# Sparse attention of a hybrid encoder: bias and mask are summed on GpSimd ahead of the logits

## The chip, the core and the metric

One NeuronCore of a Trainium2 chip runs the whole program in one launch. Its engines are TensorE (PE, matrix multiply; PEld is its weight load), VectorE (DVE), ScalarE (ACT), GpSimd (POOL) and SyncE (SP, here a queue for DMAs). Each works through its own instructions strictly in the order in which they stand in its queue, and waits on semaphores for the others. The metric is the device time of one execution in microseconds (us); the time of a version is the median of its runs.

## The reference, cut to what matters

Two layers of an encoder on a sequence of 512 positions of width 1024, all in float32. Each layer projects its normalised input with one wide matrix, feeds four mixers (a state-space scan, a sparse attention, an RWKV-7 recurrence and a diagonal state-space model called S5), gates and sums their outputs, and ends in a feed-forward block. The change lies in the sparse attention:

```python
score = jnp.where(admissible[None], score, -jnp.inf)
sel_score, sel_idx = lax.top_k(score, top_k)          # 128 keys of 512 for each query
...
logits = jnp.einsum("bqhd,bqkhd->bqhk", qb, k_sel).astype(f32) * dh ** -0.5
logits = logits + jnp.transpose(rel_bias[bucket], (0, 1, 3, 2)).astype(f32)
logits = jnp.where(valid[:, :, None, :], logits, -jnp.inf)
probs = jax.nn.softmax(logits, axis=-1)
return jnp.einsum("bqhk,bqkhd->bqhd", probs.astype(v.dtype), v_sel)
```

There are 8 heads of 64 columns. A query sees only keys of its own chunk of 64 and of earlier chunks.

## The kernel before

Nothing is gathered. The kernel computes the logits of each block of 128 queries against all keys up to the block's end, and adds a mask that holds 0 where a key is among the chosen and 1e30 where it is not. All signs are turned over (queries are scaled by -1/8, the bias is stored negated), so the softmax's maximum is a minimum here, and the exponential takes scale -1.

The function `dsa` does a layer's attention. `dsa_scores` first makes the masks of query blocks qt = 1 to 3: sixteen pairs of a MAX (L708) and a MATCH_REPLACE (L709) on DVE take the 128 largest scores of each query, and L710 writes the mask. The main loop then runs over four pairs of heads (hp) and four query blocks (qt); a step is one (hp, qt), has W = 128, 256, 384 or 512 keys, and does the two heads e = 0 and 1 of the pair. For each head:

- PE: logits into PSUM tile `lgp` (L656).
- DVE: `lg` = logits + bias (L661), then one custom operation that adds the mask and takes the row minimum `mn` (L662, TENSOR_TENSOR_REDUCE, which the trace calls CUSTOM_DVE_ANT_0 and the instruction order calls ISA).
- ACT: exponential with the row sum (L664). DVE: reciprocal (L670) and scaling (L671).
- PE: qt + 1 transposes into PSUM tile `ptp` (L674). ACT: copy of them to SBUF, `dspt` (L675). PE: product with the values, into `po` (L679).

Tiles `bias`, `lg` and some others share one ring of five buffers (tag Ta). The bias of a head is a DMA from DRAM issued by the POOL queue (L648). Logits of a step stand behind the last `po` product of the step before on PE, which the helper `behind` enforces.

The order of instructions on each engine isn't written by hand. A scheduler at build time lays out the program from priorities (attention and the other mixers stand above the large projections) and its own estimate of each operation's length. The projections fill PE wherever the mixers are not ready: `pj` (L302 to L304, three matrix multiplies for each pair of tiles, helper `mm3`) and `pgl`, the same lines used by the S5 mixer's gated unit (L1075 to L1077 are its operations on ACT and DVE). Their weights come by DMA into `raw`; ACT makes the rounded part `wh` (L295) and DVE the rest `wl` (L296). A `pj` or `pgl` multiply that stands on PE between an attention step's logits and its transposes is called a filler here.

Of the kernel before, what the change touches and what calls it, by code (L numbers as in the profile page):

```python
# [81 lines left out]
def ap_of(t, offset, dims):  # L82
    return bass.AP(tensor=t.tensor, offset=t.offset + offset, ap=[list(d) for d in dims])


class Trunk:
# [521 lines left out]
    def dsa(self, ar):  # L608
        nc = self.nc
        mm = nc.tensor.matmul  # L610
        self.misc_proj(ar)
        qs = self.A(ar + "0", [4, S], "dsq", F32R)
        qh, ql = self.T("dsqh", dt=F32R), self.T("dsql", dt=F32R)
        self.split_out(qh, ql, self.pin(C_QI))
        for j in range(4):
            for n, t in enumerate((qh, ql, qh)):
                nc.gpsimd.dma_start(qs[32 * n:32 * n + 32, j], t[32 * j:32 * j + 32])
        mask = self.mask
        moff = [0, 128, 384, 768]
        nc.gpsimd.memset(mask[:, :128], 0.0)  # L620
        nc.gpsimd.memset(mask[:64, 64:128], -NEG)
        yb = self.y_dram("ybd")
        qvs = []
        for hp in range(4):
            qv = self.A(f"{ar}{2 + hp}", [4, S], "qkvo")
            qvs.append(qv)
            q, k, vc = qv[:, 0], qv[:, 1], qv[:, 3]
            vt = qv[:, 2].rearrange("p (t c) -> p t c", c=128)
            nc.scalar.activation(q, self.pin(C_Q + hp * 128), AF.Copy, scale=-0.125)
            nc.scalar.copy(k, self.pin(C_K + hp * 128))  # L630
            nc.scalar.copy(vc, self.pin(C_V + hp * 128))
            pv = self.P("pv")
            for t in range(4):
                nc.tensor.transpose(pv[:, t * 128:(t + 1) * 128], vc[:, t * 128:(t + 1) * 128], self.ident)
            nc.scalar.copy(vt, pv.rearrange("p (t c) -> p t c", c=128))
        self.dsa_scores(qs, mask, moff)
        pts = self.A(ar + "0", [2, 2, S], "dspt")
        n, freed = 0, None
        for hp in range(4):
            qv = qvs[hp]  # L640
            q, k = qv[:, 0], qv[:, 1]
            vt = qv[:, 2].rearrange("p (t c) -> p t c", c=128)
            er = [slice(e * 64, e * 64 + 64) for e in range(2)]
            po = self.P("po")
            bias, mn, sm, rs = [], [], [], []
            for e in range(2):
                b_ = self.T("bias")
                self.q("bi").dma_start(b_, ap_of(self.relb, (hp * 2 + e) * 128 * 640 + 127, [[639, 128], [1, 512]]))  # L648
                bias.append(b_)
                for l, nm in ((mn, "mn"), (sm, "sm"), (rs, "rs")):  # L650
                    l.append(self.sp.tile([128, 4], F32, name=nm, bufs=4))
            for qt in range(4):
                W = 128 * (qt + 1)
                ps = [self.P("lgp") for _ in range(2)]
                for e in range(2):
                    i = mm(ps[e][:, :W], q[er[e], qt * 128:(qt + 1) * 128], k[er[e], :W], start=True, stop=True)  # L656
                    self.behind(i, freed)
                ts_ = [self.T("lg") for _ in range(2)]
                for e in range(2):
                    t = ts_[e]  # L660
                    nc.vector.tensor_add(t[:, :W], ps[e][:, :W], bias[e][:, 384 - 128 * qt:512])  # L661
                    nc.vector.tensor_tensor_reduce(t[:, :W], t[:, :W], mask[:, moff[qt]:moff[qt] + W], 1.0, 3e38,  # L662
                                                   op0=OP.add, op1=OP.min, accum_out=mn[e][:, qt:qt + 1])
                    nc.scalar.activation(t[:, :W], t[:, :W], AF.Exp, scale=-1.0, bias=mn[e][:, qt:qt + 1],  # L664
                                         accum_out=sm[e][:, qt:qt + 1])
                pt = pts[:, n % 2]
                n += 1
                for e in range(2):
                    t = ts_[e]
                    nc.vector.reciprocal(rs[e][:, qt:qt + 1], sm[e][:, qt:qt + 1])  # L670
                    nc.vector.tensor_scalar(t[:, :W], t[:, :W], rs[e][:, qt:qt + 1], None, op0=OP.mult)  # L671
                    pp = self.P("ptp")
                    for b in range(qt + 1):
                        nc.tensor.transpose(pp[:, b * 128:(b + 1) * 128], t[:, b * 128:(b + 1) * 128], self.ident)  # L674
                    nc.scalar.copy(pt[:, e, :W], pp[:, :W])  # L675
                freed = None
                for b in range(qt + 1):
                    for e in (1, 0):
                        i = mm(po[er[e], qt * 128:(qt + 1) * 128], vt[:, b, er[e]], pt[:, e, b * 128:(b + 1) * 128],  # L679
                               start=(b == 0), stop=(b == qt))  # L680
                        self.behind(i, freed)
                        freed = i
            t = self.T("ybt")
            nc.scalar.copy(t, po)
            self.y_store(yb, hp, t)
        self.dbg_y("yb", yb)
        return yb
# [911 lines left out]
```

## Time and profile before

| what | value |
|---|---|
| three timed runs | 2310.33, 2313.12, 2317.92 us (median 2313.12) |
| profiled execution, own time | 2318.86 us |
| its span, first to last instruction | 2317.1 us |
| PE busy | 2242.8 us, 97% of the span |
| DVE busy | 1448.4 us, 63% |
| ACT busy | 921.0 us, 40% |
| POOL busy | 103.6 us, 4% |

Busy time of PE counts a multiply from its start to the end of its pipeline, and neighbours overlap, so PE's real pace is read from starts of one multiply to the next. Attention takes place from about 175 to 365 us in the first layer and from about 1304 to 1498 us in the second.

### The profile page before, as it was taken

How to read it: one execution, taken by the hardware profiler on the slowest of the kernel's cores; microseconds unless marked ns; L12 is line 12 of the kernel's file. 1: busy time of each engine (PE TensorE's matmuls, PEld its weight loads, DVE VectorE, ACT ScalarE, POOL GpSimd, SP SyncE). 2: the span in 40 equal slices, each digit the busy share in tenths (PEclk: the TensorE clock that was granted, in tenths of full speed). 3: DMA queues.
4: the chain of work that ended last, by engine and by line, in shares of the span. 5: the costliest groups of instructions: out<-in, count | busy, mean ns of one | idle time of the engine just before them, and what ended most of it. 6: DMA issues, size and time to landing. Idle time of an engine off the chain costs nothing.

```text
span 2317.1 us, 32591 instructions
## 1 busy us (share of the span) xinstructions
PE 2242.8 (97%) x12660; PEld 1789.5 (77%) x12660; DVE 1448.4 (63%) x2676; ACT 921.0 (40%) x1455; POOL 103.6 (4%) x180
## 2 busy tenths in 40 slices
PE   6999999999999999999999999999999999999998
PEld 5777777777778888887878777687777888888786
DVE  5669867767678587543244696568668775444333
ACT  5443464244642343322233335533456333222232
POOL 3320000000000101000012000000000000000000
PEclk9999999999999999999999999999999999999999
DMA  7444552444166435433365445443333653333332
GB/s 219 114 104 128 144 170 80 116 101 124 55 205 204 119 92 166 125 97 105 111 187 150 123 124 168 123 101 105 91 110 106 222 160 91 100 97 95 89 98 86
DMA packets 429186, 290.08 MB, mean 125 GB/s; under 512 B 65024, under 2 KB 386768, under 8 KB 427432
## 3 DMA queue, kind: packets, MB, share of 16 engines
q1 hardware_dynamic: 419520, 261.45, 39.3%
q0 software_dynamic: 8512, 26.43, 4.1%
q8 instruction: 99, 1.62, 0.3%
q14 instruction: 55, 0.45, 0.1%
q10 hardware_dynamic: 1000, 0.13, 0.0%
HBM read 237.30 MB, written 51.43 MB: 125 GB/s over the span
## 4 chain that ended last, share of the span: by engine, by line
PE 81%; DVE 11%; DMA 4%; issue 2%; ACT 2%; SPq 0%; DVEq 0%; ACTq 0%; POOLq 0%
PE pj L303 16%; PE pj L304 16%; PE pj L302 16%; PE pf L304 3%; PE pf L302 3%; PE pf L303 3%; PE pb L302 3%; PE pb L303 3%; PE pb L304 3%; DVE wl L296 2%; DMA rnd<-rwrn 1%; PE lgp L656 1%; PE ptp L674 1%; PE po L679 1%; DVE score L709 1%
## 5 line engine op out<-in xcount | busy, mean ns | idle before, releaser
L302 PE MATMUL pj<-hh,wh 128*128 128x512 f32 x1888 | 750.1, 398 | 11.0 <-DVE conv L1453 4.9
L304 PE MATMUL pj<-hh,wl 128*128 128x512 f32 x1888 | 749.7, 397 | 0.4 <-DVE wl L296 0.4
L303 PE MATMUL pj<-hl,wh 128*128 128x512 f32 x1888 | 749.7, 397 | 0.1
L295 ACT CAST wh<-raw 128x1024 fp32r<-128x1024 f32 x336 | 348.6, 1037 | 922.6 <-PE pj L303 344.3
L296 DVE TENSOR_TENSOR wl<-raw,wh 128x1024 fp32r<-128x1024 f32 x336 | 405.2, 1206 | 350.8 <-ACT wh L295 348.9
L302 PEld LDWEIGHTS pj<-hh,wh 128*128 128x128 f32 x1888 | 356.3, 189 | 91.0 <-issue 8.6
L303 PEld LDWEIGHTS pj<-hl,wh 128*128 128x128 f32 x1888 | 356.4, 189 | 81.7 <-issue 9.0
L304 PEld LDWEIGHTS pj<-hh,wl 128*128 128x128 f32 x1888 | 356.0, 189 | 79.1 <-issue 6.3
L302 PE MATMUL pf<-hid,wh 128*128 128x512 f32 x352 | 137.9, 392 | 1.6 <-ACT wh L295 1.6
L304 PE MATMUL pf<-hid,wl 128*128 128x512 f32 x352 | 137.7, 392 | 0.5 <-DVE wl L296 0.5
L303 PE MATMUL pf<-hid,wh 128*128 128x512 f32 x352 | 136.9, 390 | 0.0
L302 PE MATMUL pb<-yh,wh 128*128 128x512 f32 x256 | 100.9, 394 | 0.0
L303 PE MATMUL pb<-yl,wh 128*128 128x512 f32 x256 | 100.8, 394 | 0.0
L304 PE MATMUL pb<-yh,wl 128*128 128x512 f32 x256 | 100.3, 392 | 0.0
L536 DVE TENSOR_TENSOR fa<-fa,pj 128x512 f32<-128x512 f32 x44 | 30.2, 688 | 95.3 <-PE pj L304 95.2
L533 DVE TENSOR_TENSOR fa<-pj,rb 128x512 f32<-128x512 f32 x44 | 30.4, 691 | 88.6 <-PE pj L304 88.6
L302 PEld LDWEIGHTS pf<-hid,wh 128*128 128x128 f32 x352 | 66.1, 188 | 16.8 <-ACT wh L295 3.4
L304 PEld LDWEIGHTS pf<-hid,wl 128*128 128x128 f32 x352 | 66.1, 188 | 16.0 <-DVE wl L296 2.6
L303 PEld LDWEIGHTS pf<-hid,wh 128*128 128x128 f32 x352 | 66.1, 188 | 13.4
L664 ACT ACTIVATE lg<-lg,mn 128x128 f32<-128x128 f32 (+3 forms) x64 | 35.8, 559 | 61.6 <-DVE mn L662 60.0
L302 PEld LDWEIGHTS pb<-yh,wh 128*128 128x128 f32 x256 | 48.1, 188 | 10.7 <-DVE m L476 0.7
L303 PEld LDWEIGHTS pb<-yl,wh 128*128 128x128 f32 x256 | 48.1, 188 | 9.8
(493 smaller groups left out, 2977.5 us busy)
## 6 DMA issues: line engine op xcount, KB each, us to landing
raw<-in_w_in SPq DMA_DIRECT2D x146, 512.0 KB
raw<-in_ffn_w SPq DMA_DIRECT2D x120, 512.0 KB
gates<-gate SPq DMA_DIRECT2D x64, 256.0 KB
gld<-gates SPq DMA_DIRECT2D x64, 256.0 KB
raw<-in_w_branch SPq DMA_DIRECT2D x32, 512.0 KB
raw<-in_w_out SPq DMA_DIRECT2D x16, 512.0 KB
raw<-in_ffn_w SPq DMA_DIRECT2D x16, 384.0 KB
bias<-relb POOLq DMA_DIRECT2D x16, 256.0 KB, 3.1
```

The lines of the kernel that those rows point to most:

```text
L295: nc.scalar.copy(wh[:, :n], raw[:, :n])
L296: nc.vector.tensor_sub(wl[:, :n], raw[:, :n], wh[:, :n].bitcast(F32))
L302: mm(ps, wh, ah, start=first, stop=False)
L303: mm(ps, wh, al, start=False, stop=False)
L304: mm(ps, wl, ah, start=False, stop=last)
L533: nc.vector.tensor_mul(a, p1, rb)
L536: nc.vector.tensor_mul(a, a, p3)
L656: i = mm(ps[e][:, :W], q[er[e], qt * 128:(qt + 1) * 128], k[er[e], :W], start=True, stop=True)
L664: nc.scalar.activation(t[:, :W], t[:, :W], AF.Exp, scale=-1.0, bias=mn[e][:, qt:qt + 1], accum_out=sm[e][:, qt:qt + 1])
L674: nc.tensor.transpose(pp[:, b * 128:(b + 1) * 128], t[:, b * 128:(b + 1) * 128], self.ident)
L679: i = mm(po[er[e], qt * 128:(qt + 1) * 128], vt[:, b, er[e]], pt[:, e, b * 128:(b + 1) * 128], start=(b == 0), stop=(b == qt))
L709: nc.vector.match_replace(sc[:, :W], m8, sc[:, :W], PICK)
```

## The change

The sum that no longer needs the logits goes first, and to another engine. GpSimd adds the bias and the mask into the step's `lg` tile. DVE's custom operation then adds the logits from PSUM to it and takes the minimum; DVE's own addition is gone. The sums are formed in another order, with the same operands.

```diff
                 for e in range(2):
                     t = ts_[e]
-                    nc.vector.tensor_add(t[:, :W], ps[e][:, :W], bias[e][:, 384 - 128 * qt:512])
-                    nc.vector.tensor_tensor_reduce(t[:, :W], t[:, :W], mask[:, moff[qt]:moff[qt] + W], 1.0, 3e38,
+                    nc.gpsimd.tensor_add(t[:, :W], bias[e][:, 384 - 128 * qt:512], mask[:, moff[qt]:moff[qt] + W])
+                    nc.vector.tensor_tensor_reduce(t[:, :W], ps[e][:, :W], t[:, :W], 1.0, 3e38,
                                                    op0=OP.add, op1=OP.min, accum_out=mn[e][:, qt:qt + 1])
                     nc.scalar.activation(t[:, :W], t[:, :W], AF.Exp, scale=-1.0, bias=mn[e][:, qt:qt + 1],
```

The scheduler lays the program out anew around this; outside the two stretches of attention and some 130 us behind each, the order is the same. Three places show what moves.

On POOL, the first layer. Before, the eight bias loads (two for each pair of heads) stand one behind the other:

```order
L1013 DMA s5T<-ktd 16x16x16
L648 DMA bias<-relb 128x512 x8
L1211 MEMSET NZ 64x32 x2
```

In the changed kernel the additions stand between them (here the first two pairs of heads; the ISA row is there once in the program):

```order
L648 DMA bias<-relb 128x512 x2
L661 ISA
L661 TENSOR_TENSOR lg<-bias,mask 128x128 x2
L661 TENSOR_TENSOR lg<-bias,mask 128x256 x2
L661 TENSOR_TENSOR lg<-bias,mask 128x384 x2
L661 TENSOR_TENSOR lg<-bias,mask 128x512 x2
L648 DMA bias<-relb 128x512 x2
L661 TENSOR_TENSOR lg<-bias,mask 128x128 x2
L661 TENSOR_TENSOR lg<-bias,mask 128x256 x2
```

So a pair's bias loads are issued only behind the eight additions of the pair before, and an addition stands behind the bias loads of its own pair.

On DVE, the step of 256 keys of the first layer's last pair of heads. Before:

```order
L661 TENSOR_TENSOR lg<-lgp,bias 128x256 x2
L662 ISA lg,mn<-lg,mask 128x256
L662 ISA mn 128x1
L662 ISA lg,mn<-lg,mask 128x256
L662 ISA mn 128x1
L670 RECIPROCAL rs<-sm 128x1
L671 TENSOR_SCALAR lg<-lg,rs 128x256
```

and in the changed kernel:

```order
L662 ISA lg,mn<-lgp,lg 128x256
L662 ISA mn 128x1
L662 ISA lg,mn<-lgp,lg 128x256
L662 ISA mn 128x1
L670 RECIPROCAL rs<-sm 128x1
L671 TENSOR_SCALAR lg<-lg,rs 128x256
```

Both additions went from the front of the step's chain on DVE. On PE, the same step, from the logits to the first transposes. Before:

```order
L656 MATMUL lgp<-qkvo 128x256 x2
L304 MATMUL pj<-hh,wl 128x512
L302 MATMUL pj<-hh,wh 128x512
L303 MATMUL pj<-hl,wh 128x512
L304 MATMUL pj<-hh,wl 128x512
L302 MATMUL pj<-hh,wh 128x512
L303 MATMUL pj<-hl,wh 128x512
L304 MATMUL pj<-hh,wl 128x512
L302 MATMUL pj<-hh,wh 128x512
L303 MATMUL pj<-hl,wh 128x512
L304 MATMUL pj<-hh,wl 128x512
L674 MATMUL ptp<-cst,lg 128x128 x2
```

and in the changed kernel:

```order
L656 MATMUL lgp<-qkvo 128x256 x2
L303 MATMUL pgl<-yg_2986,wh 128x512
L304 MATMUL pgl<-yg_2985,wl 128x512
L302 MATMUL pgl<-yg_2985,wh 128x512
L303 MATMUL pgl<-yg_2986,wh 128x512
L304 MATMUL pgl<-yg_2985,wl 128x512
L302 MATMUL pgl<-yg_2985,wh 128x512
L674 MATMUL ptp<-cst,lg 128x128 x2
```

Ten fillers stood between logits and transposes, and six do now. Counted in the same way over pairs of heads hp = 1, 2, 3 of both layers (six steps for each width), the fillers ahead of the first transposes are:

| keys W | before, first layer; second layer | changed, first layer; second layer |
|---|---|---|
| 256 | 10, 16, 10; 13, 10, 16 | 10, 6, 6; 6, 6, 6 |
| 384 | 10, 10, 6; 10, 15, 10 | 7, 7, 7; 7, 7, 8 |
| 512 | 28, 12, 12; 25, 12, 12 | 12, 7, 7; 9, 7, 7 |

Steps of 128 keys have 18 or more in both. Steps of the pair hp = 0 have 89, 14, 34 and 71 (W = 128 to 512) in the changed kernel's first layer, and 84, 9, 91 and 81 in its second. From the first to the second head's transposes of a step, and from there to the value products, stand one to six more fillers in most steps, in both kernels.

## Rows read from the trace of the kernel before

**Rows 1.** Page: span, and busy time and instructions of each engine.
```profile
span 2317.1 us, 32591 instructions
PE 2242.8 (97%) x12660; PEld 1789.5 (77%) x12660; DVE 1448.4 (63%) x2676; ACT 921.0 (40%) x1455; POOL 103.6 (4%) x180
```

**Rows 2.** Busy time by stretch, both attention stretches and what follows them.
```profile
core 0: us, PE busy (x) PEld busy (x) DVE busy (x) ACT busy (x) POOL busy (x), PEclk, DMA share, GB/s
175.00:500.00 325.00, 316.58 (x1865) 243.14 (x1863) 244.48 (x524) 142.94 (x251) 3.38 (x7) 1.00 0.46 127
1295.00:1620.00 325.00, 314.78 (x1674) 240.96 (x1672) 246.82 (x548) 144.00 (x251) 4.50 (x9) 0.99 0.45 125
```

**Rows 3.** Who PE waited for, whole program: total us, times, longest.
```profile
PE ptp L674 <- DVE lg L671: 8.9, 17, 1.1
```

**Rows 4.** Busy time by stretch, while DVE makes the masks.
```profile
180.00:200.00 20.00, 18.96 (x88) 14.62 (x87) 19.46 (x56) 6.52 (x13) 0.00 (x0) 1.00 0.48 142
240.00:260.00 20.00, 18.61 (x139) 14.45 (x138) 19.64 (x41) 8.27 (x12) 0.54 (x1) 1.00 0.48 142
```

**Rows 5.** DVE's groups by shape: count, busy us, mean ns, idle before.
```profile
L661 DVE TENSOR_TENSOR lg<-lgp,bias 128x512 f32<-128x512 f32 x16 | 10.9, 687 | 10.0 <-PE lgp L656 9.9
...
L661 DVE TENSOR_TENSOR lg<-lgp,bias 128x384 f32<-128x384 f32 x16 | 8.8, 553 | 8.7 <-PE lgp L656 8.7
...
L661 DVE TENSOR_TENSOR lg<-lgp,bias 128x256 f32<-128x256 f32 x16 | 6.4, 421 | 12.5 <-PE lgp L656 12.3
...
L661 DVE TENSOR_TENSOR lg<-lgp,bias 128x128 f32<-128x128 f32 x16 | 4.6, 286 | 3.0 <-PE lgp L656 3.0
```

**Rows 6.** Timeline of a 512-key step (start us, length us): DVE, then PE.
```profile
329.59 0.69 DVE L661 TENSOR_TENSOR lg<-lgp,bias 128x512 f32<-128x512 f32 x1 [0.25 <-PE lgp L656]
330.32 0.69 DVE L662 CUSTOM_DVE_ANT_0 lg<-lg,mask 128x512 f32<-128x512 f32 x1
...
330.06 0.40 PE L303 MATMUL pgl<-yg,wh 128*128 128x512 f32 x1
...
332.12 0.39 PE L303 MATMUL pj<-hl,wh 128*128 128x512 f32 x1
333.01 0.66 PE L674 MATMUL ptp<-cst,lg 128*128 128x128 f32 x4 [0.50 <-DVE lg L671]
```

**Rows 7.** Timeline of a 384-key step: DVE, then PE.
```profile
321.22 0.56 DVE L661 TENSOR_TENSOR lg<-lgp,bias 128x384 f32<-128x384 f32 x1 [1.05 <-PE lgp L656]
321.81 0.56 DVE L662 CUSTOM_DVE_ANT_0 lg<-lg,mask 128x384 f32<-128x384 f32 x1
...
323.29 0.39 PE L303 MATMUL pgl<-yg,wh 128*128 128x512 f32 x1
324.03 0.44 PE L674 MATMUL ptp<-cst,lg 128*128 128x128 f32 x2 [0.35 <-DVE lg L671]
```

**Rows 8.** Timeline of a 256-key step, all engines in order of start.
```profile
346.03 0.76 DVE L661 TENSOR_TENSOR lg<-lgp,bias 128x256 f32<-128x256 f32 x2 [2.07 <-PE lgp L656]
...
346.71 0.41 DVE L662 CUSTOM_DVE_ANT_0 lg<-lg,mask 128x256 f32<-128x256 f32 x1
...
348.11 0.39 PE L304 MATMUL pj<-hh,wl 128*128 128x512 f32 x1
...
348.41 0.44 PE L674 MATMUL ptp<-cst,lg 128*128 128x128 f32 x2
```

**Rows 9.** Timeline of PE, first transposes of one step to the next step's logits.
```profile
290.32 0.55 PE L674 MATMUL ptp<-cst,lg 128*128 128x128 f32 x3 [0.36 <-DVE lg L671]
...
293.17 1.13 PE L656 MATMUL lgp<-qkvo 64*128 64x512 f32 x4
```

**Rows 10.** POOL's groups by shape: memsets by columns.
```profile
L176 POOL MEMSET sm<- 128x512 f32 x1 | 0.5, 543 | 0.0
...
L620 POOL MEMSET mask<- 128x128 f32 x2 | 0.4, 208 | 227.7 <-PE pf L304 222.2 <-PE xtp L221 5.5
```

**Rows 11.** All instructions on tile bias: its DMAs, issue to landing.
```profile
DMA to landing us min/median/max: 2.9/3.1/4.6
```

**Rows 12.** DVE's groups by shape: two operations that read SBUF twice or fast.
```profile
L296 DVE TENSOR_TENSOR wl<-raw,wh 128x1024 fp32r<-128x1024 f32 x318 | 388.8, 1223 | 289.5 <-ACT wh L295 287.5 <-PE ptp L674 0.9
...
L671 DVE TENSOR_SCALAR lg<-lg,rs 128x512 f32<-128x512 f32 x16 | 7.8, 486 | 0.5
```

## The prediction

> **What bounds the kernel now.** The page's busy times come first: PE works for 2242.8 of 2317.1 us, and no other engine for more than two thirds of it [rows 1]. The stretches come next: in the two that the change touches, PE is busy for 316.58 and 314.78 of 325 us, which leaves 8.42 and 10.22 us, 18.6 us in all, that anything here can win back [rows 2]. Of these, the list of waits puts 8.9 us, in 17 waits of at most 1.1 us, on transposes that wait for DVE's scaled exponentials [rows 3]. That is the end of the very chain that the change shortens. The reader is to see two things: the kernel is bound by TensorE's total work, which the change leaves as it is, and only TensorE's idle time can change the result. While the masks are made DVE is nearly full (19.46 and 19.64 of 20 us) and yet PE misses only 1.04 and 1.39 us of each 20 [rows 4], because the projections fill it.
>
> **What is removed.** DVE's 64 additions, 10.9 + 8.8 + 6.4 + 4.6 = 30.7 us [rows 5]. As DVE time I cost them at nothing: PE's fillers cover DVE. Without that cover they'd be worth up to 30.7 us, but there is no more than the 18.6 us to win.
>
> What counts is the chain from logits to transposes. In the 512-key step the minimum starts 330.32 - 329.59 = 0.73 us behind the addition; take that away, and the chain ends 0.73 us earlier [rows 6]. With 384 keys it is 321.81 - 321.22 = 0.59 us [rows 7]; with 256, where both heads' additions stand ahead of the first minimum, 346.71 - 346.03 = 0.68 us [rows 8].
>
> **What moves.** The scheduler knows that the chain became shorter and puts the transposes earlier on PE. A filler is worth its start-to-start time: from 330.06 to 332.12 there are nine, so 0.23 us each [rows 6]. I compare cover and chain for each width:
>
> - 512 keys: the last filler starts at 332.12, so PE could have gone on at 332.35; the transposes start at 333.01. Idle now: 0.66 us [rows 6]. Twelve fillers become seven, 5 x 0.23 = 1.15 us less cover, against 0.73 us less chain: 1.08 us idle.
> - 384 keys: 324.03 - 323.52 = 0.51 us idle now [rows 7]. Ten become seven, 0.69 us against 0.59: 0.61 us.
> - 256 keys: 348.41 - 348.34 = 0.07 us idle now [rows 8]. Ten become six, 0.92 us against 0.68: 0.31 us.
>
> So the scheduler takes away more cover than the chain gives back. The sum over the three pairs of heads behind the first and both layers, with the filler counts of the changed order: 512 keys, four steps at seven fillers (1.08 each), one at nine (0.62), one at twelve (0): 4.94 us. 384 keys: five at 0.61, one with eight fillers at 0.38: 3.43 us. 256 keys: five at 0.31, one that keeps ten and loses its idle time: 1.55 us. Together 9.9 us. The same working for the order of before, six steps of each width at 0.66, 0.51 and 0.07, gives 7.4 us, where the trace has 8.9 [rows 3]; the longer covers there stand where ACT or DVE was held up by other work. **Change: +2.5 us.** Fillers that are not used here are not lost: they run later, and PE's total stays.
>
> The second head costs nothing on either side: behind its transposes' predecessors stand one or two fillers, as long as the spacing of the two exponentials.
>
> **What is added.** GpSimd's 64 additions. The trace has no addition on GpSimd. The nearest rows are its memsets: 0.543 us for 512 columns, 0.208 us for 128 [rows 10]. A memset writes alone, so one of the same width is the lower end. For the upper end I take three passes, two reads and a write, one after the other: 1.63 us for 512 columns. I work with the upper end, since a sum of two tiles is nearest to that. It still costs nothing where it is ahead of the logits. The tightest place is the pair hp = 1: with five buffers in the ring, an addition there has to wait until the step before has transposed the tile that it reuses. In the step of [rows 9] that is 290.32 + 0.55 = 290.87; the logits of the next end at 293.17 + 1.13 = 294.30, and the second head's minimum comes behind the first's, which takes some 0.69 us. With one filler less in between that leaves 294.99 - 290.87 - 0.23 = 3.9 us for two additions, 2 x 1.63 = 3.26. Behind hp = 1 the tiles come free a step earlier. The bias loads, now between the additions, take 3.1 us to land [rows 11]; they serve the 128-key steps, which have 18 fillers or more (4.1 us) on top of the value products. The mask's last step waits for one more addition, 1.63 us at most, under 71 and 81 fillers (16 us or more). The single ISA row has no price in the trace; 89 fillers, some 20 us, lie over it. An addition that is late would hold DVE's minimum, and behind it on DVE the next `wl`, on which PE's projections wait.
>
> A rule speaks against putting the addition there. The Trainium skill, GPSIMD Engine Reference, § 4.1 Engine selection, sends elementwise additions to VectorE, because GpSimd is about two times slower with two inputs. Its § 3.1 measures 4497 ns for 2048 columns; an estimate by that page is 1.12 us for 512, which the 3.9 us hold twice, so the sum would stay +2.5 us. No run here shows it yet.
>
> **Rivals.**
>
> 1. *The shorter chain wins.* Other work in front of the chain on DVE and ACT shrinks too, and the transposes' waits vanish: at most the 8.9 us of [rows 3], 2318.9 - 8.9 = 2310.0 us in terms of the profiled execution. For it: DVE is full in [rows 4] and loses work. Against it: the scheduler's smaller cover. Chance 0.17.
> 2. *The addition comes late.* It decides from 3.9 / 2 = 1.95 us for an addition of 512, over my upper end. At 2.5 us each, two would be 5.0 - 3.9 = 1.1 us late in each of the six steps of hp = 1, 7 us more than the sum. Chance 0.15.
> 3. *DVE and GpSimd hold each other up.* DVE runs operations with two SBUF inputs all the time (`wl`, 1.22 us), and the scaling of the chain itself takes 0.486 us for 512 columns, less than the 0.687 us of an addition of that width, so it runs in a faster mode [rows 5, 12]. If one of them has to wait for a GpSimd addition in each of the 18 steps, for half of an addition's 1.1 us on the mean (three memsets of 0.38 us, the mean of 512 and 128 columns), that is 18 x 0.55 = 10 us more than the sum. Chance 0.18. Against it: the additions fall mostly between two steps' chains, and DVE's new minimum reads PSUM and only one SBUF tile. The Trainium skill, SBUF — State Buffer, § Who interferes with whom, states such a lock: an operation of DVE with two SBUF inputs, or in a two-port mode, and a GpSimd operation that reads SBUF block each other until the first is done. The trace of before has no compute of GpSimd there to show it.
>
> **How the numbers follow.** The profiled execution took 2318.86 us, of which 2317.1 are its span; the median of the runs is 2313.12, 5.7 us less. The likeliest case is 2318.9 + 2.5 = 2321.4 us there, so 2316 us for a median. Its own range is 2310 to 2321, chance 0.50. Rival 1 gives 2304, rival 2 gives 2323, rival 3 gives 2326. The range of 2304 to 2328 takes them in. The runs of before spread by 0.3%, about 7 us, and less than that a measurement of this kernel can't tell from no change. The likeliest case falls within it; of rival 1 nearly all is faster, of rivals 2 and 3 nearly all slower: 0.16 faster, 0.55 same, 0.29 slower.
>
> **What would show it right or wrong.** Right: in the profile after, DVE's busy time is some 31 us lower, POOL's 24 to 72 us higher, PE's the same; transposes wait for DVE for about 10 us in more waits than 17; an addition of 512 takes 0.54 to 1.63 us; DVE's minimum waits for `lgp` and hardly ever for POOL. Wrong: transposes that wait well under 6 us (rival 1), minima that wait for POOL's `lg` (rival 2), or DVE's `wl` and scaling longer than 1.22 and 0.486 us (rival 3). A shift of idle time behind the attention, in the RWKV part, would also upset the sum: I took it as unchanged.

## The result and the profile after

| what | before | changed |
|---|---|---|
| median of the runs (4 each) | 2313.28 us (2310.33 to 2317.92) | 2327.63 us (2326.45 to 2328.99) |
| ratio, 95% interval | | 1.0065 (1.0052 to 1.0078) |
| profiled execution, own time and span | 2318.86, 2317.1 us | 2326.45, 2324.3 us |

The changed kernel is slower by some 14 us. Two more comparisons, told below, gave 1.0033 (1.0021 to 1.0046) and 1.0062 (1.0042 to 1.0082): slower each time, by a size that isn't settled better than 8 to 16 us.

The page of the changed kernel, to be read beside [rows 1]:

```profile
span 2324.3 us, 32663 instructions
PE 2242.7 (96%) x12660; PEld 1789.8 (77%) x12660; DVE 1434.1 (62%) x2612; ACT 922.0 (40%) x1455; POOL 172.7 (7%) x244
```

PE's work is the same. DVE has lost 64 instructions that took 30.7 us [rows 5], and yet its busy time fell by 14.3 us only. So other operations on DVE became longer. By how much isn't the plain difference of 16.4 us: spans of neighbours on DVE overlap (in [rows 8] the minimum starts at 346.71, while the two additions end at 346.79). Counted in the trace of before, DVE is busy with nothing but one of these additions for 25.4 us, and with everything else for 1423.0. So the other operations became 11.1 us longer. That difference is the first thing that the reader should stop at.

The two stretches of attention, as in [rows 2]:

```profile
core 0: us, PE busy (x) PEld busy (x) DVE busy (x) ACT busy (x) POOL busy (x), PEclk, DMA share, GB/s
175.00:500.00 325.00, 310.98 (x1765) 239.51 (x1764) 237.31 (x493) 138.79 (x241) 35.22 (x39) 0.99 0.45 125
1295.00:1620.00 325.00, 312.87 (x1642) 239.69 (x1641) 235.42 (x503) 143.37 (x250) 41.38 (x41) 0.99 0.45 124
```

PE is busy for 5.6 and 1.9 us less than before, 7.5 us. The list of PE's waits names the place, as in [rows 3]:

```profile
PE ptp L674 <- DVE lg L671: 15.9, 26, 2.1
...
PE s5py L1031 <- DVE s5xs L1023: 5.9, 4, 2.3
...
PE ptp L674 <- DVE rs L670: 2.2, 3, 1.7
```

Transposes wait 18.1 us where they waited 8.9. The S5 mixer's `s5py` adds 1.0 us (4.9 before). DVE's groups by shape show which of its operations grew (count, busy us, mean ns, idle before):

```profile
L296 DVE TENSOR_TENSOR wl<-raw,wh 128x1024 fp32r<-128x1024 f32 x318 | 392.2, 1233 | 309.9 <-ACT wh L295 308.6 <-DMA x<-xd 0.2
...
L662 DVE CUSTOM_DVE_ANT_0 lg<-lgp,lg 128x512 f32<-128x512 f32 x16 | 10.7, 689 | 23.1 <-PE lgp L656 19.1 <-POOL lg L661 4.0
...
L1076 DVE SCALAR_TENSOR_TENSOR glt<-glt,yg 128x512 f32<-128x512 f32 x8 | 8.1, 1010 | 0.1
...
L671 DVE TENSOR_SCALAR lg<-lg,rs 128x512 f32<-128x512 f32 x16 | 7.7, 485 | 0.5
...
L1077 DVE TENSOR_SCALAR glt<-glt 128x512 f32<-128x512 f32 x8 | 6.1, 761 | 0.2
```

The same two groups of the gated unit before the change:

```profile
L1076 DVE SCALAR_TENSOR_TENSOR glt<-glt,yg 128x512 f32<-128x512 f32 x8 | 5.5, 686 | 3.9 <-ACT glt L1075 3.9
L1077 DVE TENSOR_SCALAR glt<-glt 128x512 f32<-128x512 f32 x8 | 3.4, 424 | 0.2
```

The minimum, which now reads PSUM and one tile of SBUF, takes what it took. `wl` (L296) and L1076 read two tiles of SBUF; L1077 reads one, in 0.424 us against 0.686, so in a faster mode. These three grew by 3.4, 2.6 and 2.7 us, 8.7 of the 11.1 us; L1017, a subtraction of the S5 mixer with two SBUF inputs, adds 0.8 (1.22 to 1.42 us on the mean of four). The scaling (L671), fast too, kept its 0.485 us for 512 columns: no addition met it there. GpSimd's additions grew too, where they met them. POOL's groups by shape:

```profile
L661 POOL TENSOR_TENSOR lg<-bias,mask 128x512 f32<-128x512 f32 x16 | 24.4, 1532 | 93.6 <-DVE mask L710 86.9 <-PE ptp L674 6.2
...
L661 POOL TENSOR_TENSOR lg<-bias,mask 128x128 f32<-128x128 f32 x16 | 9.4, 590 | 65.6 <-PE ptp L674 32.6 <-DVE mask L710 30.9 <-DVE lg L671 2.2
```

The worst single wait shows the whole mechanism. It is a timeline of the 384-key step of the second layer's last pair of heads, POOL and DVE, then PE:

```profile
1481.41 4.93 POOL L661 TENSOR_TENSOR lg<-bias,mask 128x384 f32<-128x384 f32 x3 [2.47 <-PE ptp L674]
1481.71 1.80 DVE L296 TENSOR_TENSOR wl<-raw,wh 128x1024 fp32r<-128x1024 f32 x1 [0.38 <-ACT wh L295]
1483.43 1.75 DVE L1076 SCALAR_TENSOR_TENSOR glt<-glt,yg 128x512 f32<-128x512 f32 x1
1485.22 1.41 DVE L1077 TENSOR_SCALAR glt<-glt 128x512 f32<-128x512 f32 x1
1486.55 0.55 DVE L662 CUSTOM_DVE_ANT_0 lg<-lgp,lg 128x384 f32<-128x384 f32 x1
...
1483.48 0.92 PE L656 MATMUL lgp<-qkvo 64*128 64x384 f32 x4
...
1486.06 0.39 PE L302 MATMUL pgl<-yg,wh 128*128 128x512 f32 x1
1488.55 0.55 PE L674 MATMUL ptp<-cst,lg 128*128 128x128 f32 x3 [2.10 <-DVE lg L671]
```

The transposes of the step before free buffers of the ring, and GpSimd starts three additions: one for this step's second head, and two for the 512-key step behind it. DVE needs none of them before 1487 us. On DVE `wl` takes 1.80 us instead of 1.22, L1076 1.75 instead of 0.69, and L1077 1.41 instead of 0.42: 2.63 us in all. They stand ahead of the minimum in DVE's queue. The logits end at 1484.40 and the minimum starts at 1486.55, and PE, whose fillers end, waits 2.10 us.

A 512-key step that no addition meets looks like this in the changed kernel (DVE, then PE):

```profile
322.88 0.69 DVE L662 CUSTOM_DVE_ANT_0 lg<-lgp,lg 128x512 f32<-128x512 f32 x1 [2.22 <-PE lgp L656]
...
324.46 0.16 DVE L670 RECIPROCAL rs<-sm 128x1 f32<-128x1 f32 x1 [0.27 <-ACT lg L664]
...
325.20 0.66 PE L674 MATMUL ptp<-cst,lg 128*128 128x128 f32 x4 [0.62 <-DVE lg L671]
```

### The profile page after: what moved, and what is told of

It reads as the page before. It is cut to its first block, busy times and chain, and to the rows that moved or that the text cites. A ratio compares the mean times of both kernels' runs of the same rounds, so it can differ in the third digit from the quotient of the medians.

```text
span 2324.3 us, 32663 instructions
## 1 busy us (share of the span) xinstructions
PE 2242.7 (96%) x12660; PEld 1789.8 (77%) x12660; DVE 1434.1 (62%) x2612; ACT 922.0 (40%) x1455; POOL 172.7 (7%) x244
## 4 chain that ended last, share of the span: by engine, by line
PE 75%; DVE 10%; issue 6%; DMA 4%; ACT 2%; POOL 1%; SPq 0%; DVEq 0%; ACTq 0%; POOLq 0%
PE pj L303 15%; PE pj L302 15%; PE pj L304 15%; PE pf L304 3%; PE pf L303 3%; PE pf L302 3%; PE pb L302 3%; PE pb L303 3%; PE pb L304 3%; DVE wl L296 2%; PE ptp L674 1%; PE po L679 1%; PE lgp L656 1%; PE rwA L1186 1%; DVE score L709 1%
## 5 line engine op out<-in xcount | busy, mean ns | idle before, releaser
L302 PE MATMUL pj<-hh,wh 128*128 128x512 f32 x1888 | 749.9, 397 | 10.5 <-DVE conv L1453 4.3
L296 DVE TENSOR_TENSOR wl<-raw,wh 128x1024 fp32r<-128x1024 f32 x336 | 408.6, 1216 | 371.3 <-ACT wh L295 370.0
L661 POOL TENSOR_TENSOR lg<-bias,mask 128x128 f32<-128x128 f32 (+3 forms) x64 | 68.7, 1085 | 261.8 <-DVE mask L710 142.8
L533 DVE TENSOR_TENSOR fa<-pj,rb 128x512 f32<-128x512 f32 x44 | 30.4, 690 | 88.5 <-PE pj L304 88.5
L662 DVE CUSTOM_DVE_ANT_0 lg<-lgp,lg 128x128 f32<-128x128 f32 (+3 forms) x64 | 29.6, 486 | 46.6 <-PE lgp L656 41.5
```

The source lines that it names most:

```text
L296: nc.vector.tensor_sub(wl[:, :n], raw[:, :n], wh[:, :n].bitcast(F32))
L302: mm(ps, wh, ah, start=first, stop=False)
L533: nc.vector.tensor_mul(a, p1, rb)
L661: nc.gpsimd.tensor_add(t[:, :W], bias[e][:, 384 - 128 * qt:512], mask[:, moff[qt]:moff[qt] + W])
L662: nc.vector.tensor_tensor_reduce(t[:, :W], ps[e][:, :W], t[:, :W], 1.0, 3e38, op0=OP.add, op1=OP.min, accum_out=mn[e][:, qt:qt + 1])
```

## The experiments

Two theories stood against each other at first: the scheduler's shorter cover (the prediction's likeliest case), and the lock between DVE and GpSimd (its rival 3). The table gives every kernel that ran. "DVE longer" is the time for which DVE is busy with anything but the additions of L661, counted in the trace, over the 1423.0 us of before (in e6_glu_act without L1077 too, over 1420.1); the changed kernel has 11.1. The waits are those of transposes in the list of PE's waits; the changed kernel has 18.1, the kernel before 8.9.

| run | ratio to before (95%) | DVE longer, us | transposes wait, us |
|---|---|---|---|
| before, once more (e0_again) | 0.9994 (0.998 to 1.0008) | 0.5 | 8.8 |
| addition ahead of the logits, on DVE (e1_dve_preadd) | 1.0003 (0.999 to 1.0017) | 0.3 | 8.0 |
| before, with side addition (e2_side_add) | 1.0051 (1.0035 to 1.0066) | 19.3 | 16.5 |
| before, with memsets of the tile (e3_tile_memset) | 1.0006 (0.9992 to 1.002) | 0.1 | 10.7 |
| before, with two side additions (e4_side_twice) | 1.0182 (1.0161 to 1.0204) | 40.8 | 37.1 |
| changed, additions in pieces (e5_pieces) | 1.0067 (1.0049 to 1.0085) | 6.1 | 21.4 |
| changed, L1077 on ACT (e6_glu_act) | 1.0051 (1.0031 to 1.0071) | 8.3 | 16.1 |
| before, with side copy (e8_side_copy) | 0.9999 (0.9985 to 1.0014) | 1.8 | 9.1 |
| changed, again (e7_after_again) | 1.0033 (1.0021 to 1.0046) | 11.4 | 17.9 |
| changed, third time (e11_after_third) | 1.0062 (1.0042 to 1.0082) | 11.6 | 19.4 |
| changed, GpSimd for hp = 0 only (e9_first_pair) | 1.0007 (0.9997 to 1.0018) | 2.7 | 10.6 |
| changed, GpSimd for hp = 1 to 3 only (e10_other_pairs) | 1.0006 (0.9995 to 1.0017) | 4.4 | 13.0 |

**e0_again** is the kernel before, as a yardstick.

> The kernel of before once more, with a second profile, to tell how far its executions and its waits spread. Both theories: 2313 us within 5 us; PE waits for the transposes about 9 us.

Measured: 2310.53 us, span 2306.3. So the profiled execution of before, 2317.1 us, was one of the longer ones, and only parts of two traces, not their spans, should be compared.

**e1_dve_preadd** leaves the addition where the change puts it and gives it back to DVE.

```diff
-                    nc.gpsimd.tensor_add(t[:, :W], bias[e][:, 384 - 128 * qt:512], mask[:, moff[qt]:moff[qt] + W])
+                    nc.vector.tensor_add(t[:, :W], bias[e][:, 384 - 128 * qt:512], mask[:, moff[qt]:moff[qt] + W])
```

> The changed kernel with its addition of bias and mask on DVE instead of GpSimd, still ahead of the logits. The order on PE keeps the short covers (6, 7, 7 fillers in most steps). Theory of the cover (the scheduler takes away more cover than the chain gives back): most of the loss stays, transposes wait 13 to 16 us, 2318 to 2322 us. Theory of the lock (GpSimd's additions and DVE's operations hold each other up): no GpSimd, so no loss; transposes wait 9 to 10 us, 2313 us.

Measured: 2311.21 us, as before. Its fillers ahead of the transposes are nearly as few as in the changed kernel: 6 or 7 in 12 of the 18 steps of 256 to 512 keys behind the first pair, where that has 14 such steps and the kernel before has one. PE's waits:

```profile
PE ptp L674 <- DVE lg L671: 8.0, 16, 1.8
```

The theory of the cover falls: the new order without GpSimd's work loses nothing that can be measured (3.9 us at most by the interval), and its transposes wait no longer than before.

**e2_side_add** is the opposite half: the kernel before, with GpSimd doing the same additions beside it, into columns that nobody reads. The mask's tile is made wider for that.

```diff
-        self.mask = self.A(ar + "1", [1280], "mask")
+        self.mask = self.A(ar + "1", [2048], "mask")
...
+                    nc.gpsimd.tensor_add(mask[:, 1280:1280 + W], bias[e][:, 384 - 128 * qt:512], mask[:, moff[qt]:moff[qt] + W])
                     nc.vector.tensor_add(t[:, :W], ps[e][:, :W], bias[e][:, 384 - 128 * qt:512])
```

> The kernel of before with GpSimd's 64 additions beside it, into columns of the mask's tile that nobody reads. The order on PE, DVE and ACT is that of before. Theory of the lock: DVE's operations with two SBUF inputs take up to 1.3 us longer, transposes wait 4 to 6 us more than the 9 of before, 2317 to 2321 us. Theory of the cover: nothing changes, 2313 us.

Measured: 2323.06 us against 2311.0. The order on PE, DVE and ACT is that of before, nobody uses the sums, and the loss is there. The additions don't lie quite where the changed kernel has them: behind the first pair, a pair's additions wait for no buffer of the ring and run back to back behind its bias loads, as here on POOL:

```profile
274.36 7.00 POOL L661 TENSOR_TENSOR mask<-bias,mask 128x128 f32<-128x128 f32 x7 [0.28 <-DMA bias<-relb]
```

The page:

```profile
PE 2238.3 (97%) x12660; PEld 1784.9 (77%) x12660; DVE 1467.7 (63%) x2676; ACT 921.5 (40%) x1455; POOL 172.4 (7%) x244
```

And the list of PE's waits:

```profile
PE ptp L674 <- DVE lg L671: 16.1, 21, 2.5
```

DVE is busy 19.3 us longer with the same 2676 instructions. Here the minimum reads two tiles of SBUF, and it grew as well (0.690 to 0.893 us for 512 columns), so this kernel is more exposed than the changed one.

**e3_tile_memset** asks whether any work of GpSimd does it, or the wait for it. The kernel before, with two memsets of the step's `lg` tile ahead of DVE's addition:

```diff
+                    nc.gpsimd.memset(t[:, :W], 0.0)
+                    nc.gpsimd.memset(t[:, :W], 0.0)
                     nc.vector.tensor_add(t[:, :W], ps[e][:, :W], bias[e][:, 384 - 128 * qt:512])
```

> The kernel of before with two GpSimd memsets of the step's tile ahead of DVE's addition, about as long as an addition on GpSimd, but writing only. Theory of the lock, if it is the reading that counts: DVE's operations keep their lengths, 2313 to 2315 us. If any work of GpSimd slows DVE, or if the wait for GpSimd's tile is the cost: as the run with the side additions, 2317 to 2321 us. Theory of the cover: 2313 us.

Measured: 2315.17 us, ratio 1.0006, within what can't be told from no change. POOL's groups and DVE's:

```profile
L661 POOL MEMSET lg<- 128x512 f32 x32 | 16.9, 534 | 80.9 <-PE ptp L674 59.5 <-DVE rs L670 17.2 <-DMA ybd<-ybt 2.1
...
L1076 DVE SCALAR_TENSOR_TENSOR glt<-glt,yg 128x512 f32<-128x512 f32 x8 | 5.5, 686 | 3.9 <-ACT glt L1075 3.9
```

GpSimd works 45 us more than before, ahead of the same tiles and between the same bias loads, and DVE isn't longer in sum. (Of its fast operations, L1077 grew from 0.424 to 0.446 us and the scaling of 384 columns from 0.418 to 0.448, on the mean; `wl` and L1076 kept their lengths.) So writing, waiting in the ring and the order of the bias loads make no loss that can be measured at this dose; additions, which also read, do.

**e4_side_twice** doubles the dose of e2_side_add.

```diff
+                    nc.gpsimd.tensor_add(mask[:, 1280:1280 + W], bias[e][:, 384 - 128 * qt:512], mask[:, moff[qt]:moff[qt] + W])
                     nc.gpsimd.tensor_add(mask[:, 1280:1280 + W], bias[e][:, 384 - 128 * qt:512], mask[:, moff[qt]:moff[qt] + W])
```

> The kernel before, with the side addition on GpSimd issued twice for each tile (into unused columns of a widened mask tile; the result isn't used). Order on PE, DVE and ACT as before. Theory (GpSimd's reading of SBUF blocks DVE's operations that read SBUF twice or fast): twice the reading, so twice what one side addition cost: about 2 x 12 = 24 us over the kernel before, 2335 us where it is 2311; DVE's busy time about 38 us over 1449; POOL's about 240 us. Rival (what costs is that the first addition of a pair comes at a bad place, or the bias loads behind it come late, and the rest is hidden): the loss stays near 12 us, 2323, and DVE's busy time near 1468. Second rival (saturation: GpSimd runs out of time and DVE's minimum isn't concerned): waits of DVE for POOL stay under 2 us.

Measured: 2352.04 against 2312.43 us. DVE's lengthening doubles (19.3 to 40.8 us), as the theory wants; the time lost more than triples (12 to 40 us), which the theory didn't expect. A cover that hides part of one dose and not of two would explain it; that wasn't tested. The timeline of a 128-key step, whose transposes then wait 5.27 us:

```profile
319.07 7.92 POOL L661 TENSOR_TENSOR mask<-bias,mask 128x384 f32<-128x384 f32 x5
...
320.89 1.37 DVE L662 CUSTOM_DVE_ANT_0 lg<-lg,mask 128x128 f32<-128x128 f32 x1
...
322.40 2.13 DVE L296 TENSOR_TENSOR wl<-raw,wh 128x1024 fp32r<-128x1024 f32 x1
324.46 1.35 DVE L662 CUSTOM_DVE_ANT_0 lg<-lg,mask 128x128 f32<-128x128 f32 x1
...
325.92 1.15 DVE L671 TENSOR_SCALAR lg<-lg,rs 128x128 f32<-128x128 f32 x1
326.99 0.15 DVE L670 RECIPROCAL rs<-sm 128x1 f32<-128x1 f32 x1
327.18 0.29 DVE L671 TENSOR_SCALAR lg<-lg,rs 128x128 f32<-128x128 f32 x1
...
327.22 0.45 PE L674 MATMUL ptp<-cst,lg 128*128 128x128 f32 x1 [5.27 <-DVE rs L670]
```

While additions run, a minimum takes 1.37 us and a scaling 1.15; behind the last one a scaling takes 0.29. The reciprocal, one column, isn't touched.

**e5_pieces** cuts each of the changed kernel's additions into pieces of 128 columns.

```diff
-                    nc.gpsimd.tensor_add(t[:, :W], bias[e][:, 384 - 128 * qt:512], mask[:, moff[qt]:moff[qt] + W])
+                    [nc.gpsimd.tensor_add(t[:, c:c + 128], bias[e][:, 384 - 128 * qt + c:512 - 128 * qt + c], mask[:, moff[qt] + c:moff[qt] + c + 128]) for c in range(0, W, 128)]
```

> The changed kernel with each addition on GpSimd cut into pieces of 128 columns; fillers ahead of the transposes as in the changed kernel. Theory A (a blocked DVE operation waits for the one addition that runs, however long it is; the length of one hold counts): a piece takes some 0.45 us undisturbed against 1.27 for 512, so a DVE operation is held for at most about 0.45 us at a time; DVE's busy time comes down from 1434 towards 1425, transposes wait for DVE some 11 us instead of 18, and the time falls to about 2317 to 2321 where the kernel before takes 2311. Theory B (what counts is the total time for which GpSimd reads SBUF while DVE wants to): 160 pieces of 0.45 to 0.59 us are 72 to 94 us against 68.7, so no gain: 2326 to 2330, DVE's busy time 1434 or more.

Measured: 2326.79 us. Theory A had DVE right (1429.1 us, 6.1 longer instead of 11.1) and the time wrong; theory B had the time right and DVE wrong. POOL's group of additions:

```profile
L661 POOL TENSOR_TENSOR lg<-bias,mask 128x128 f32<-128x128 f32 x160 | 88.5, 582 | 253.2 <-DVE mask L710 137.0 <-PE ptp L674 86.7 <-DMA ybd<-ybt 19.6
```

And DVE's waits for them:

```profile
DVE lg L662 <- POOL lg L661: 8.1, 8, 1.9
```

The pieces take 88.5 us where the whole additions took 69.1, and the minimum now waits 8.1 us for them instead of 4.8. Transposes wait 21.4 us instead of 18.1. Additions that end later are the likely reason why DVE's gain doesn't show in the time; no run isolates it.

**e6_glu_act** takes one of the held operations off DVE.

```diff
-            nc.vector.tensor_scalar(t, t, 0.5, None, op0=OP.mult)
+            nc.scalar.mul(t, t, 0.5)
```

> The changed kernel with the halving of the S5 mixer's gated unit (L1077, on DVE in a fast mode, 0.42 us alone and up to 1.41 beside GpSimd's additions) on ACT instead. Theory (many DVE operations are each held a little; wl with its 318 executions above all): only the eight halvings are spared, at most 8 x 0.34 = 2.7 us on DVE, so the time stays within 3 us of the changed kernel: 2323 to 2328 where the kernel before takes 2311. Rival (the few gated unit operations that stand in the chain make most of the loss, the waits of 1.9 and 2.1 us among them): the loss falls by half or more, to 2318 or less, and the longest wait of transposes to under 1.2 us.

Measured: 2322.5 against 2312.43 us. The longest wait of a transpose is 2.2 us, as long as before this edit, and most of the loss stayed, so L1077 alone isn't its cause. Whether it is worth a part of it is inconclusive: the ratio lies between those of the changed kernel's three comparisons.

**e8_side_copy** puts a copy, which reads one tile, in the place of e2_side_add's addition.

```diff
+                    nc.gpsimd.tensor_copy(mask[:, 1280:1280 + W], bias[e][:, 384 - 128 * qt:512])
```

> The kernel before, with a copy of the bias on GpSimd beside each step (one input from SBUF, one output into unused columns; the result isn't used) instead of a side addition. Order on PE, DVE and ACT as before. If any reading of SBUF by GpSimd blocks DVE: the loss goes with the copies' time on POOL; at half of the additions' time it is about 6 us, 2317 where the kernel before takes 2311, and DVE's busy time some 9 us over 1449. If only an operation of GpSimd with two inputs blocks: no loss, 2309 to 2313, and DVE's busy time 1448 to 1450, as beside the memsets.

Measured: 2311.55 us, no loss. POOL's group, and DVE's minimum of 128 columns, which takes 0.282 us in the kernel before:

```profile
L661 POOL COPY mask<-bias 128x512 f32<-128x512 f32 x16 | 11.9, 744 | 1.0
...
L662 DVE CUSTOM_DVE_ANT_0 lg<-lg,mask 128x128 f32<-128x128 f32 x16 | 5.7, 353 | 0.2
```

The second expectation, no loss, fits the time; DVE's 1450.2 us lie a little over its edge, and the minimum of 128 columns is held somewhat. The copies take 39.2 us, over half of the additions' 69, and hold DVE for 1.8 us against 19.3. So the lock isn't simply GpSimd's time. A copy does hold DVE: here the second head's minimum of 128 columns takes 0.70 us instead of 0.28, while copies run.

```profile
337.92 1.29 POOL L661 COPY mask<-bias 128x512 f32<-128x512 f32 x2
338.66 0.70 DVE L662 CUSTOM_DVE_ANT_0 lg<-lg,mask 128x128 f32<-128x128 f32 x1
```

But `wl` kept its 1.222 us, and the copies were held up instead: one took 1.67 us, where the shortest of its width took 0.61. Whether the second input, the shorter single operation or which of the two engines started first makes the difference, this run doesn't tell.

**e7_after_again** and **e11_after_third** are the changed kernel, unaltered.

> The changed kernel once more, for a second profile of it. Theory (the loss has two parts: idle time of TensorE that comes back in every execution, since the order and the lock are the same, and a lower granted clock behind the longest waits, which need not come every time): about 2325 to 2328 where the kernel before takes 2311; waits of transposes for DVE again 17 to 19 us in all, against some 9 for the kernel before; the two waits of 1.9 and 2.1 us in the 384-key steps of the last pair of heads again, and behind them stretches of some 3 us with a granted clock near 0.5. Rival (the waits of the first profile were an accident of one execution): waits of 9 to 12 us, and no such stretch in the attention.

> The changed kernel a third time. Its two ratios so far are 1.0065 (1.0052 to 1.0078) and 1.0033 (1.0021 to 1.0046), with the same waits in both profiles. If the size differs from chip to chip, or from call to call: a ratio between 1.002 and 1.009 that need not agree with either; the profile again has 17 to 19 us of transposes' waits for DVE and about 5 us lost to a lower clock in the attention. If the first ratio was the accident: 1.002 to 1.005.

Measured: 2320.57 against 2312.84 us, and 2325.87 against 2310.16. The waits come back in both (17.9 and 19.4 us, the longest 2.1). The lower clock doesn't come back in both; the last section tells of it.

**e9_first_pair** and **e10_other_pairs** divide the additions between GpSimd and DVE, by the pair of heads.

```diff
-                    nc.gpsimd.tensor_add(t[:, :W], bias[e][:, 384 - 128 * qt:512], mask[:, moff[qt]:moff[qt] + W])
+                    (nc.gpsimd if hp == 0 else nc.vector).tensor_add(t[:, :W], bias[e][:, 384 - 128 * qt:512], mask[:, moff[qt]:moff[qt] + W])
```

In the second the two engines are exchanged.

> The changed kernel with the additions of the first pair of heads (hp = 0, while DVE makes the masks) on GpSimd, and those of the three other pairs on DVE, ahead of the logits as in the changed kernel. Theory (GpSimd's reading costs where it meets DVE's operations with two SBUF inputs; MAX and MATCH_REPLACE beside it weren't lengthened): a quarter of the additions, mostly beside MAX and MATCH_REPLACE, cost almost nothing: 2309 to 2314 where the kernel before takes 2311, DVE's busy time 1441 to 1446 (7.7 us less than 1449, and a few back), no stretch of lower clock in the attention. Rival 1 (the loss goes with GpSimd's time wherever it lies): a quarter of some 14 us, 2314 to 2316, and DVE's busy time at 1445 or more. Rival 2 (DVE is full while the masks are made, so what GpSimd takes off it there is a gain): 2300 to 2307.

> The other half of the division: the additions of the pairs hp = 1, 2, 3 on GpSimd, those of the first pair on DVE, all ahead of the logits. Theory (the loss arises where GpSimd's additions meet the short steps behind the masks, with wl and the gated unit's operations around them): the loss of the whole change within 2 us, with waits of transposes for DVE of 14 to 18 us, one or two of them near 2 us in the 384-key steps of the last pair of heads or at their place, and stretches of lower clock in the attention. Rival (the loss goes with GpSimd's time wherever it lies, or the first pair's additions make the long covers that matter): three quarters of the changed kernel's loss or less, waits under 12 us, no such stretch.

Measured: 2313.96 against 2312.84 us and 2313.14 against 2310.16, neither to be told from before. The first fits the theory, though its interval (0.7 us below to 4.2 above) doesn't exclude rival 1's 3.6 us. Its minimum waits for GpSimd 4.8 us, as long as in the changed kernel; in e10_other_pairs it doesn't wait for GpSimd at all. So the additions that come late are those of the first pair, and their lateness costs little or nothing. The second went against the theory: three quarters of the additions, in the very steps where the waits were, and no loss that can be measured. The two groups of the gated unit in e10_other_pairs show a part of why:

```profile
L1076 DVE SCALAR_TENSOR_TENSOR glt<-glt,yg 128x512 f32<-128x512 f32 x8 | 5.6, 704 | 2.5 <-ACT glt L1075 2.5
...
L1077 DVE TENSOR_SCALAR glt<-glt 128x512 f32<-128x512 f32 x8 | 4.2, 530 | 0.2
```

In the changed kernel they take 1010 and 761 ns. The scheduler, given another program, put other operations beside the additions. In the middle of their intervals the two halves add up to 1.0013, and to 5.8 us more waits, where the whole change has 1.0033 to 1.0065, and 9.0 to 10.5 us. The loss doesn't look like a sum over additions, then, though the upper ends of the two intervals add up to 1.0035, more than the smallest of the three ratios. That it depends on which operations of DVE the order sets beside them is the reading that is left; it wasn't isolated by a run.

## Why the prediction was wrong

- **What bounds the kernel** held. PE's total stayed (2242.8 and 2242.7 us busy), and the loss shows as idle time ahead of transposes.
- **What is removed and moves** was mis-sized. I let the chain end 0.73 us earlier in a 512-key step. But the second head's addition had stood ahead of the first head's reciprocal on DVE as well. From the first operation on the logits to the transposes it was 333.01 - 329.59 = 3.42 us [rows 6], and is 325.20 - 322.88 = 2.32 now: 1.10 us less. With 1.15 us less cover that leaves 0.66 + 1.15 - 1.10 = 0.71 us idle, 0.05 more than before, where I had 1.08, 0.42 more. The wait that the trace itself names there, counted from the end of the last filler, went from 0.50 [rows 6] to 0.62. So the term of +2.5 us doesn't show: e1_dve_preadd has nearly this order without GpSimd's work, and its transposes wait 8.0 us, less than the 8.9 of before. Its time alone, with an interval up to 3.9 us, couldn't exclude 2.5.
- **What is added** was where it failed. The duration was right: two undisturbed additions of 512 take 2.63 us below, 1.3 each, within the 0.54 to 1.63 us given. It also came in time nearly always: the minimum waited for it in 6 waits, 4.8 us, as the list of DVE's waits below says. The step that failed is "It still costs nothing where it is ahead of the logits". I looked for its cost only in its own lateness, and it lay in what GpSimd does to DVE's other work meanwhile: 11.1 us longer on DVE, 9.2 us more waits of transposes.

```profile
288.81 2.63 POOL L661 TENSOR_TENSOR lg<-bias,mask 128x512 f32<-128x512 f32 x2 [3.13 <-PE ptp L674]
...
DVE lg L662 <- POOL lg L661: 4.8, 6, 1.5
```

- **Rival 3 is what happened**, at a chance of 0.18. Its price of 10 us is near the 9.2 us that transposes wait longer, and its 2326 us near the 2327.63. That the numbers fit is in part luck: the 2326 holds the 2.5 us of cover that don't show, and the price was half an addition in each of 18 steps, where the holds fall on a few `wl` and the gated unit ahead of some minima. Both arguments against it were true and didn't matter. The additions do fall between two steps' chains, and the minimum isn't lengthened; but DVE fills just that time with `wl` and the gated unit, which stand ahead of the minimum. The Trainium skill, SBUF — State Buffer, § Who interferes with whom, says that a DVE operation with two SBUF inputs contends with a GpSimd operation that reads SBUF, not with one that only writes; that a DVE operation in a two-port mode contends with GpSimd; that whichever issues first holds the shared ports for the whole instruction; and that a DVE operation with one SBUF input at most, outside those modes, doesn't contend. The runs agree: L1076 0.69 to 1.75 us, L1077 0.42 to 1.41, an unchanged minimum (0.689) on PSUM and one tile, and L1076 unchanged beside memsets (0.686). Beside copies, which read SBUF with one input, there are holds too, but only 1.8 us of them in sum (e8_side_copy).
- **Rivals 1 and 2** didn't come: waits grew, and late additions held the minimum for 4.8 us, all of it in the first pair, where e9_first_pair has the same 4.8 us and no loss that can be measured.
- **What would show it**, as far as it was named, did: DVE's 14.3 us instead of 31 (25.4 would have been right for operations that don't grow), `wl` at 1.80 us, waits of 18 us.

The waits of transposes explain 9.2 us, and that for `s5xs` 1.0. What the rest of some 14 us is in the first comparison, and why another comparison gave 8, stays open.

## What to carry to other kernels

Before work is given to GpSimd "for free", look at what DVE runs at that time: if it reads two SBUF tiles or runs in a fast mode there, price each addition by what it holds up, ahead of the operation that the critical engine waits for. If DVE's busy time falls by clearly less than the removed instructions took, overlaps of neighbours allowed for, look for the operations that grew. Two experiments settle such a case: the moved work back on its old engine in the new order, and the same work as an unused extra in the old order.

## What the runs showed of the hardware that was not expected

The lock also works backwards: GpSimd's additions were held up by DVE. All instructions of the changed kernel's line 661 (duration in ns, least, median and most):

```profile
L661 POOL TENSOR_TENSOR lg<-bias,mask x64: 449/1010/2267, 188.7 to 1484.7; 128x128 f32<-128x128 f32 x16, 128x256 f32<-128x256 f32 x16, 128x384 f32<-128x384 f32 x16, 128x512 f32<-128x512 f32 x16
```

The longest, of 512 columns, took 2.27 us where an undisturbed one takes 1.3. MAX and MATCH_REPLACE, which read one tile, took as long beside additions as without (0.56 and 0.54 us for 384 columns).

Behind some of TensorE's long waits its granted clock fell to the lower of its two levels (1.2 GHz). Busy time by stretch of the changed kernel, from the end of a wait of 1.91 us at 345.15 us on:

```profile
345.15 0.55 PE L674 MATMUL ptp<-cst,lg 128*128 128x128 f32 x3 [1.91 <-DVE lg L671]
...
345.00:346.00 1.00, 0.85 (x5) 0.58 (x5) 0.72 (x4) 1.00 (x4) 0.00 (x0) 1.00 0.64 246
346.00:347.00 1.00, 1.00 (x5) 0.99 (x5) 0.97 (x2) 0.27 (x1) 0.00 (x0) 0.52 0.00 0
347.00:348.00 1.00, 1.00 (x3) 0.37 (x2) 0.06 (x1) 0.48 (x1) 0.00 (x0) 0.50 0.06 25
348.00:349.00 1.00, 1.00 (x9) 0.88 (x10) 0.00 (x0) 0.00 (x0) 0.00 (x0) 0.50 0.62 238
```

In this execution it happened three times in the attention, twice behind waits of transposes and once behind the 2.25 us for `s5xs`; in e7_after_again three times behind partly other waits, at a ratio of 1.0033; in e11_after_third never, and that had 1.0062 all the same. In the attention of the kernel before it wasn't seen. So it adds to single stalls, but it isn't shown to be a cause of the loss.
